# Scan scores as two 64-row products side by side instead of one 128-row product with zeros

## The chip, the core and the metric

One core of a Trainium2 chip runs the whole program. The metric is the device time of one execution in microseconds (us); the number compared is the median of several runs. TensorE is called PE, its weight loads PEld, VectorE is DVE, ScalarE is ACT, GpSimd is POOL and SyncE, which issues the DMAs, is SP.

## The reference, cut to what matters

The program is two layers of a diffusion backbone over 512 latent tokens and 256 context tokens of width 1024: SwiGLU blocks around a token mixer, RWKV-7 in the first layer and Hyena in the second. The change touches the recurrence of RWKV-7 alone. It has 16 heads of 64 channels, and runs once forwards and once backwards:

```python
def step(S, inp):
    w_t, k_t, v_t, kk_t, ka_t = inp[:5]
    sa = jnp.einsum('dbhvk,dbhk->dbhv', S, kk_t)
    S = S * w_t[..., None, :] - sa[..., None] * ka_t[..., None, :] + v_t[..., None] * k_t[..., None, :]
    if r is None:
        return S, None
    return S, jnp.einsum('dbhvk,dbhk->dbhv', S, inp[5])
```

Everything is in float32.

## The kernel before, in words

The recurrence is done in chunks of 64 tokens. Within a chunk the steps become small matrices: for each head, all products of a scaled kk or r at one token with a scaled ka or k at another, called scores here, the inverse of a triangular matrix made of them, and the state carried from chunk to chunk. `rwkv_prep` writes the scaled vectors to DRAM (`S_A` from the tile `AR`, `S_K` from `KD`), and `rwkv_scan` reads them back and does the rest.

- The 12 chunks (4 of context, then 8 latent) are taken two at a time as a block, for each of two directions d: 12 blocks. The 16 heads are two groups g of 4 pairs of heads (index `p_`). One block has thus 4 items (g and chunk), and the scan has 48 items.
- `load(i)` (L1124) fetches for one block and group the tiles `AG` (kk and r side) and `KK` (ka and k side). In both, a pair of heads takes the 128 partitions, one head in each half (`hr[0]`, `hr[1]`). In `AG` each head hh has columns of its own, and its values stand in the partitions of its half; the other half is filled with zeros (L1140 on ACT for the first `NZ` = 4 loads, L1142 on POOL for the other 20, two instructions each). A 128x4 memset (L1136, POOL) for loads 2 to 9 sets the place in the order from which such a load may go. There are 10 buffers of `AG`.
- `stage_a` (L1191) makes the scores of one item: for each of the 4 pairs one matmul (L1211) with `KK` as the weights, 128 rows by 128 columns, and both heads' columns of `AG` streaming; the zeros keep the heads apart. For a latent chunk `ns` is 2 (kk and r) and 256 columns stream; for a context chunk `ns` is 1 and 128 do. So there are 32 items with 256 columns and 16 with 128. The hardware runs each float32 matmul as two instructions, each with its weight load.
- The scores lie in PSUM: in a tile `sc` of two banks of a pool with one buffer, or, in the 11 items that are scored ahead of the first solve (`lead`), two times out of three in one of the two banks of `ps`. `evac` then has ACT copy them: half a tile to `Bc` (L1219), the other half over the zeros of `AG` (L1187), and part to `Hu` (L1187); POOL masks the last two with an affine select (L1188).
- From `Bc` DVE inverts the triangles (L1240, L1258 to L1278, L1290, L1308) with small matmuls L1317 and L1328 in between. Per item then come `rhs` (L1357, L1365), `solve` (L1372), `advance` (L1382, L1388, L1395), `carry` (POOL L1348 scales the state `Sn`, DVE L1350 copies it into `SV`) and `keys` (transposes, L1174).
- The loop at the end of `rwkv_scan` sets the order: at step n it issues solve, rhs, the scores of the item LA = 11 steps ahead, pieces of inversions, advance and so on. PE and DVE keep this written order throughout the scan, POOL while n is negative; ACT, SP and later POOL are ordered by the scheduler from its own estimate.

Of the kernel before, what the change touches and what calls it, by code (L numbers as in the profile page):

```python
# [9 lines left out]
F32 = mybir.dt.float32  # L10
F32R = mybir.dt.float32r
I32 = mybir.dt.int32
AF = mybir.ActivationFunctionType
# [5 lines left out]
P = 128  # L19
# [7 lines left out]
NP = 4  # L27
# [20 lines left out]
NVEC = 2  # L48
NL = 0
ML = {ET.PE, ET.DVE, ET.Pool}  # L50
NZ = 4
NLD = 2
FIRST = {"AG", "KK", "Bc", "L", "Dl"}
NBG = (1, 1, 2)
# [222 lines left out]
class K:  # L277
# [819 lines left out]
    def rwkv_scan(self, cx, po):  # L1097
        nc = self.nc

        pools = [self.pool(n, 1, cx) for n in ("sfirst", "schk")]  # L1100
        hr = [slice(0, 64), slice(64, P)]
# [4 lines left out]
        def T(shape, tag, bufs=1):  # L1106
            return pools[tag not in FIRST].tile(shape, F32, tag=tag, name=self.nm(tag), bufs=bufs)
# [18 lines left out]
        def load(i):  # L1126
            t, g = pairs[i]
            d = t["d"]
            ch = min(t["chs"])
            x = (g, d, ch // 6)  # L1130
            c = slice(ch % 6, ch % 6 + 2)
            AG = T([P, 2, 2, NP, 2, 64], "AG", RING)
            KK = T([P, 2, NP, 2, 64], "KK", 2)

            if NLD <= i < RING:
                nc.gpsimd.memset(AG[:, :, :, 0, 0, 0:1], 0.0)  # L1136
            for hh in range(2):
                z = AG[hr[1 - hh], :, hh].rearrange("p c a s t -> p c (a s t)")
                if i < NZ:
                    nc.scalar.activation(z, self.ones[hr[1 - hh]].unsqueeze(2).to_broadcast([64, 2, NP * P]), AF.Copy, scale=0.0)  # L1140
                else:
                    nc.gpsimd.memset(z, 0.0)  # L1142
                nc.sync.dma_start(
                    AG[hr[hh], :, hh].rearrange("p c a s t -> p c (a s t)"),
                    self.S_A[x][c, hr[hh]].rearrange("c p a s t -> p c (a s t)"),
                )
            nc.sync.dma_start(
                KK.rearrange("p c a s t -> p c (a s t)"), self.S_K[x][c].rearrange("c p a s t -> p c (a s t)")
            )
            t.setdefault("ld", {})[g] = (ch, AG, KK)  # L1150
# [35 lines left out]
        def causal(dst, src, d, ns, base):  # L1186
            nc.scalar.copy(dst, src)  # L1187
            nc.gpsimd.affine_select(  # L1188
                out=dst, in_=dst, compare_op=ALU.is_ge, fill=0.0, base=base,
                pattern=[[0, NP], [1, ns], [1 if d == 0 else -1, 64]], channel_multiplier=-1 if d == 0 else 1,  # L1190
            )  # L1191


        def stage_a(t, g, ci, lead):
            d = t["d"]
            ch = t["chs"][ci]
            ch0, AG, KK = t["ld"][g]
            c = ch - ch0
            u = 2 * g + ci
            ns = 2 if ch < 8 else 1  # L1200
            if u == 0:
                t["Bc"] = T([P, 4, NP, 64], "Bc", 3)
                t["ops"] = {}
            Bc = t["Bc"]
            Hu = T([P, NP, 64], "Hu", RKT) if ns == 2 else None
            if lead and count[0] % 3:
                sc = self.ps().rearrange("p (a h s t) -> p a h s t", a=NP, h=2, s=1)
            else:
                sc = self.psc.tile([P, NP, 2, 2, 64], F32, tag="sc", name=self.nm("sc"))
            for p_ in range(NP):  # L1210
                nc.tensor.matmul(  # L1211
                    sc[:, p_, :, :ns, :], KK[:, c, p_].rearrange("p s t -> p (s t)"), AG[:, c, :, p_, :ns, :],
                    start=True, stop=True,
                )
            t["ops"][g, ci] = (AG[:, c], Hu)

            def evac(hh):
                h_, o_ = hr[hh], hr[1 - hh]
                nc.scalar.copy(Bc[h_, u], sc[h_, :, hh, 0, :])  # L1219
                causal(AG[o_, c, hh, :, :ns], sc[o_, :, hh, :ns, :], d, ns, -1)  # L1220
                if ns == 2:
                    causal(Hu[h_].unsqueeze(2), sc[h_, :, hh, 1:2, :], d, 1, 0)

            for hh in range(2):
                ev.append(lambda hh=hh: evac(hh))
# [306 lines left out]
        count = [0, 0]  # L1532

        def scores(lead):
            x = next(nxt, None)
            if x is not None:
                count[0] += 1
                while count[1] < 2 * N and 2 * count[1] < count[0] + LDA:
                    load(count[1])
                    count[1] += 1  # L1540
                stage_a(*x, lead)


        def item(n, ahead=0):
            k, c = divmod(n, 4)
            d, g = divmod(c, 2)
            pos = k - d + ahead
            return (lines[d][pos][0], g, lines[d][pos][1]) if 0 <= pos < M and n >= 0 else None

        while count[1] < NLD:  # L1550
            load(count[1])
            count[1] += 1
# [5 lines left out]
        for n in range(-LA, 4 * M + 5):  # L1558
# [8 lines left out]
            p, x = item(n - 1), item(n)  # L1567
# [41 lines left out]
            if (n + IO) % 4 == UQ and block(n + IO):  # L1609
                t = block(n + IO)  # L1610
# [3 lines left out]
            if (n + LA + 1) % 4 == 0 and block(n + LA):  # L1614
                t = block(n + LA)
# [509 lines left out]
```

## Time and profile before

| what | value |
|---|---|
| median of 3 runs | 3029.62 us (3029.31 to 3033.85) |
| the profiled execution: its own time | 3036.99 us |
| the profiled execution: its span, first to last instruction | 3035.0 us |
| mean granted clock of TensorE in it | 0.947 |
| busy share of PE, DVE, ACT, POOL | 92%, 60%, 38%, 16% |
| the scan, first score to the start of the last inversion | about 1004 to 1381 us of the span |

A busy share is a mean over stages: the blocks before and after the scan are long streams of matmuls, in which PE alone counts. The scan is another kind of stage, and is read by itself, from windows cut out of the span. A granted clock of 1.0 is 2.4 GHz, 0.5 is 1.2 GHz; a number between is a mean over time at both.

### The profile page before, as it was taken

Reading aid. Unit: us, or ns where it says so; the run is one execution under the profiler, and the core shown is the slowest. Engines: PE = TensorE matmul, PEld = TensorE weight load, DVE = VectorE, ACT = ScalarE, POOL = GpSimd, SP = SyncE. Lnnn points to the kernel's source line nnn. Section 1 sums busy time; section 2 is a strip of 40 time slices with the busy share of each in tenths; the row PEclk is TensorE's granted clock in tenths of the full one; section 3 lists DMA queues with packets and bytes.
Section 4 is the critical chain, followed back from the end, with each engine's and each line's share of the span. In section 5 each row is a group of like instructions: output and inputs, shape, how many; then the busy total and the mean of one; then the engine's idle time right before and its main releaser. Section 6 shows DMA issues by size and latency. Waiting matters only on the chain.

```text
span 3035.0 us, 46673 instructions
## 1 busy us (share of the span) xinstructions
PE 2782.4 (92%) x18394; PEld 2324.9 (77%) x18394; DVE 1818.3 (60%) x3403; ACT 1163.4 (38%) x2007; POOL 477.7 (16%) x647
## 2 busy tenths in 40 slices
PE   8899999978889378887899999999999989899998
PEld 4788888857666366765788889888887777888888
DVE  4656444474798688997655546455365588653334
ACT  3221121255666678874232223322334322332222
POOL 0000000032343445532100000000000054100000
PEclk9999999979989678998899999999999999999999
DMA  5434333313688744434345543455333544232331
GB/s 206 155 106 148 132 128 109 100 37 102 171 211 209 192 117 130 125 86 125 128 146 167 171 162 112 140 183 180 106 116 135 206 143 147 105 124 85 97 106 48
DMA packets 363971, 409.36 MB, mean 135 GB/s; under 512 B 77719, under 2 KB 303127, under 8 KB 362024
## 3 DMA queue, kind: packets, MB, share of 16 engines
q1 hardware_dynamic: 363752, 406.39, 42.4%
q8 instruction: 144, 2.36, 0.3%
q14 instruction: 75, 0.61, 0.1%
HBM read 340.20 MB, written 65.34 MB: 134 GB/s over the span
## 4 chain that ended last, share of the span: by engine, by line
PE 74%; DVE 13%; DMA 4%; ACT 3%; issue 3%; POOL 2%; SPq 0%; DVEq 0%; POOLq 0%; ACTq 0%
PE ps L481 21%; PE ps L482 21%; PE ps L483 21%; DVE Dl L1278 1%; PE sc L1211 1%; DVE wlo L487 1%; DVE Tm L1271 1%; DMA mraw<-in_mod_wt 1%; DVE SV L1350 1%; DVE zt L1946 1%; POOL za L1947 1%; DVE zl L487 1%; PE pf L1759 1%; DMA AG<-S_A 1%; DMA x<-in_xT 1%
## 5 line engine op out<-in xcount | busy, mean ns | idle before, releaser
L482 PE MATMUL ps<-hl,whi 128*128 128x512 f32 (+1 forms) x2064 | 742.4, 362 | 3.5 <-DVE hl L268 3.5
L481 PE MATMUL ps<-hh,whi 128*128 128x512 f32 (+1 forms) x2064 | 732.2, 363 | 14.2 <-ACT hh L267 10.7
L483 PE MATMUL ps<-hh,wlo 128*128 128x512 f32 (+1 forms) x2064 | 735.6, 362 | 2.0 <-DVE wlo L487 2.0
L487 DVE TENSOR_TENSOR wlo<-raw,whi 128x1024 fp32r<-128x1024 f32 (+1 forms) x325 | 392.9, 1215 | 383.6 <-ACT whi L486 382.6
L486 ACT CAST whi<-raw 128x1024 fp32r<-128x1024 f32 (+1 forms) x338 | 344.6, 1028 | 707.8 <-PE ps L482 631.2
L481 PEld LDWEIGHTS ps<-hh,whi 128*128 128x128 f32 x2064 | 386.7, 190 | 78.3 <-ACT hh L267 13.2
L482 PEld LDWEIGHTS ps<-hl,whi 128*128 128x128 f32 x2064 | 392.8, 190 | 64.4 <-DVE hl L268 4.9
L483 PEld LDWEIGHTS ps<-hh,wlo 128*128 128x128 f32 x2064 | 391.8, 190 | 63.4 <-DVE wlo L487 2.9
L481 PE MATMUL ps<-dh,whi 128*128 128x512 f32 (+1 forms) x1072 | 354.3, 336 | 7.8 <-DVE x L660 7.8
L482 PE MATMUL ps<-dl,whi 128*128 128x512 f32 (+1 forms) x1072 | 358.3, 335 | 0.0
L483 PE MATMUL ps<-dh,wlo 128*128 128x512 f32 (+1 forms) x1072 | 357.8, 335 | 0.0
L421 DVE CUSTOM_DVE_ANT_0 mraw<-mraw,mc 128x1024 f32<-128x1024 f32 x128 | 156.5, 1223 | 142.8 <-DMA mraw<-in_mod_wt 141.6
L481 PEld LDWEIGHTS ps<-dh,whi 128*128 128x128 f32 x1072 | 203.5, 190 | 29.4 <-DVE x L660 8.0
L482 PEld LDWEIGHTS ps<-dl,whi 128*128 128x128 f32 x1072 | 204.2, 190 | 20.5
L483 PEld LDWEIGHTS ps<-dh,wlo 128*128 128x128 f32 x1072 | 204.0, 190 | 20.2
L375 POOL COPY mraw<-dl 128x1 f32<-128x1 f32 x128 | 44.8, 364 | 896.3 <-DVE dl L487 631.2
L611 DVE TENSOR_TENSOR sg<-sg,ps 128x512 f32<-128x512 f32 (+1 forms) x110 | 69.1, 633 | 175.6 <-PE ps L483 165.5
L610 ACT ACTIVATE sg<-ps 128x512 f32<-128x512 f32 (+1 forms) x110 | 59.8, 553 | 209.7 <-PE ps L483 202.8
L486 ACT CAST dh<-sg 128x512 fp32r<-128x512 f32 (+1 forms) x110 | 62.1, 575 | 201.2 <-DVE sg L611 201.1
L482 PE MATMUL ps<-xl,whi 128*128 128x512 f32 (+2 forms) x336 | 125.8, 376 | 9.6 <-DVE xl L811 7.1
L481 PE MATMUL ps<-xh,whi 128*128 128x512 f32 (+2 forms) x336 | 123.6, 380 | 9.5 <-issue 5.9
L483 PE MATMUL ps<-xh,wlo 128*128 128x512 f32 (+2 forms) x336 | 123.2, 372 | 0.0
(315 smaller groups left out, 4498.6 us busy)
## 6 DMA issues: line engine op xcount, KB each, us to landing
raw<-in_wgu SPq DMA_DIRECT2D x88, 1024.0 KB, 5.0
mraw<-in_mod_wt SPq DMA_DIRECT2D x128, 512.0 KB, 5.3
raw<-in_wd SPq DMA_DIRECT2D x24, 1024.0 KB, 5.0
raw<-in_wrkv SPq DMA_DIRECT2D x12, 1024.0 KB, 5.9
S_A<-AR SPq DMA_DIRECT2D x32, 384.0 KB, 3.6
AG<-S_A SPq DMA_DIRECT2D x48, 256.0 KB, 4.2
KK<-S_K SPq DMA_DIRECT2D x24, 512.0 KB, 4.5
KL<-S_K SPq DMA_DIRECT2D x48, 256.0 KB, 2.9
```

What stands on the lines that cost most here:

```text
L375: self.nc.gpsimd.tensor_copy(raw[:, :1], held)
L421: nc.vector.tensor_tensor_reduce(dst, raw, self.rows[w], 1.0, 0.0, ALU.mult, ALU.add, accum_out=cols[w][:, m : m + 1])
L481: nc.tensor.matmul(out, wh, xh, start=start, stop=False)
L482: nc.tensor.matmul(out, wh, xl, start=False, stop=False)
L483: nc.tensor.matmul(out, wl, xh, start=False, stop=stop)
L486: self.nc.scalar.copy(hi, src)
L487: (self.nc.gpsimd if pool else self.nc.vector).tensor_tensor(lo, src, hi.bitcast(F32), ALU.subtract)
L610: nc.scalar.activation(sg, pg, AF.Silu)
L611: nc.vector.tensor_mul(sg, sg, pu)
L1211: nc.tensor.matmul(sc[:, p_, :, :ns, :], KK[:, c, p_].rearrange("p s t -> p (s t)"), AG[:, c, :, p_, :ns, :], start=True, stop=True,)
L1271: nc.vector.tensor_tensor(tm[:, js, rs], L[:, p, rs].unsqueeze(1).to_broadcast([P, n, w]), Dl[:, js, p : p + 1].to_broadcast([P, n, w]), A ...
L1278: nc.vector.tensor_tensor(Dl[:, js, rs], Dl[:, js, rs], tm[:, js, rs], ALU.subtract)
```

## The change

The zeros are no longer written. Each score product becomes two, one for each head: 64 rows of `KK` as weights (still 128 columns) and that head's 64 rows of `AG` streaming. The two heads use different row halves of PE's array and write to different PSUM banks. In `sc` the bank is now the head; ahead of the first solve every second item takes both banks of `ps` and the others take `sc`.

```diff
-NZ = 4
             for hh in range(2):
-                z = AG[hr[1 - hh], :, hh].rearrange("p c a s t -> p c (a s t)")
-                if i < NZ:
-                    nc.scalar.activation(z, self.ones[hr[1 - hh]].unsqueeze(2).to_broadcast([64, 2, NP * P]), AF.Copy, scale=0.0)
-                else:
-                    nc.gpsimd.memset(z, 0.0)
                 nc.sync.dma_start(
...
-            if lead and count[0] % 3:
-                sc = self.ps().rearrange("p (a h s t) -> p a h s t", a=NP, h=2, s=1)
+
+            if lead and count[0] % 2:
+                sc = [self.ps().rearrange("p (a s t) -> p a s t", a=NP, s=2) for _ in range(2)]
             else:
-                sc = self.psc.tile([P, NP, 2, 2, 64], F32, tag="sc", name=self.nm("sc"))
+                sc = self.psc.tile([P, 2, NP, 2, 64], F32, tag="sc", name=self.nm("sc"))
+                sc = [sc[:, hh] for hh in range(2)]
             for p_ in range(NP):
-                nc.tensor.matmul(
-                    sc[:, p_, :, :ns, :], KK[:, c, p_].rearrange("p s t -> p (s t)"), AG[:, c, :, p_, :ns, :],
-                    start=True, stop=True,
-                )
+                for hh in range(2):
+                    nc.tensor.matmul(
+                        sc[hh][:, p_, :ns, :], KK[hr[hh], c, p_].rearrange("p s t -> p (s t)"),
+                        AG[hr[hh], c, hh, p_, :ns, :], start=True, stop=True,
+                    )
...
-                nc.scalar.copy(Bc[h_, u], sc[h_, :, hh, 0, :])
-                causal(AG[o_, c, hh, :, :ns], sc[o_, :, hh, :ns, :], d, ns, -1)
+                nc.scalar.copy(Bc[h_, u], sc[hh][h_, :, 0, :])
+                causal(AG[o_, c, hh, :, :ns], sc[hh][o_, :, :ns, :], d, ns, -1)
                 if ns == 2:
-                    causal(Hu[h_].unsqueeze(2), sc[h_, :, hh, 1:2, :], d, 1, 0)
+                    causal(Hu[h_].unsqueeze(2), sc[hh][h_, :, 1:2, :], d, 1, 0)
```

The change moves instructions at the start of the scan, where the scheduler and the PSUM buffers decide. In the changed kernel all line numbers after `load` are lower by 3 to 6 (L1211 is L1208 there).

PE, the first scores; `pq` are products of the end of the preparation, `ps` and `sc` scores, and the number after the underscore is the tile. Before:

```order
L1211 MATMUL ps_8339<-AG_8322,KK_8323 128x128 x4
L1211 MATMUL ps_8350<-AG_8322,KK_8323 128x128 x4
L1075 MATMUL pq_8282<-rb_8253,rks_8283 128x384
L1075 MATMUL pq_8282<-r_8094,rks_8283 128x384
L1211 MATMUL sc_8361<-AG_8329,KK_8330 128x2x64 x4
```

and in the change:

```order
L1074 MATMUL pq_8282<-rb_8253,rks_8283 128x384
L1074 MATMUL pq_8282<-r_8094,rks_8283 128x384
L1208 MATMUL ps_8335<-AG_8322,KK_8323 128x64
L1208 MATMUL ps_8336<-AG_8322,KK_8323 128x64
L1208 MATMUL ps_8335<-AG_8322,KK_8323 128x64
L1208 MATMUL ps_8336<-AG_8322,KK_8323 128x64
L1208 MATMUL ps_8335<-AG_8322,KK_8323 128x64
L1208 MATMUL ps_8336<-AG_8322,KK_8323 128x64
L1208 MATMUL ps_8335<-AG_8322,KK_8323 128x64
L1208 MATMUL ps_8336<-AG_8322,KK_8323 128x64
L1208 MATMUL sc_8351<-AG_8322,KK_8323 128x64 x8
```

The last `pq` products now stand ahead of the first scores, one item takes both `ps` tiles, and the next takes `sc`. In the steady part of the scan PE's order is the same, with 8 matmuls where 4 stood.

SP, the DMAs around the first load (`AG` and `KK` are loads of the scan; `S_A`, `S_K` and `S_b` are the last writes of the preparation). Before:

```order
L1143 DMA AG_8322<-S_A_4902 64x2x512
L1058 DMA S_A_4905<-AR_8250 128x6x128
L1065 DMA S_K_4913<-KD_8255 64x6x64
L1143 DMA AG_8322<-S_A_4902 64x2x512
L1147 DMA KK_8323<-S_K_4910 128x2x512
L1143 DMA AG_8329<-S_A_4906 64x2x512
L1079 DMA S_b<-rb_8150 128x128
L1143 DMA AG_8329<-S_A_4906 64x2x512
```

and in the change:

```order
L1137 DMA AG_8322<-S_A_4902 64x2x512
L1078 DMA S_b<-rb_8150 128x128
L1057 DMA S_A_4905<-AR_8250 128x6x128
L1064 DMA S_K_4913<-KD_8255 64x6x64
L1062 DMA S_K_4913<-KD_8255 64x6x128
L1064 DMA S_K_4913<-KD_8255 64x6x64
L1137 DMA AG_8322<-S_A_4902 64x2x512
L1141 DMA KK_8323<-S_K_4910 128x2x512
```

The second half of the first `AG` load and its `KK` have moved behind `S_b` and two more writes of `S_K`.

## Rows read from the trace of the kernel before

**Rows 1.** The page: the chain that ended last, shares of the span by engine.

```profile
PE 74%; DVE 13%; DMA 4%; ACT 3%; issue 3%; POOL 2%; SPq 0%; DVEq 0%; POOLq 0%; ACTq 0%
```

**Rows 2.** Windows of the scan: length, busy PE, PEld, DVE, ACT, POOL, then PEclk, DMA.

```profile
993.00:1069.00 76.00, 35.56 (x348) 32.13 (x348) 47.08 (x152) 47.57 (x102) 30.57 (x62) 0.63 0.67 182
...
1131.00:1193.00 62.00, 51.17 (x782) 41.78 (x780) 53.80 (x162) 49.52 (x110) 31.31 (x50) 0.83 0.43 122
1193.00:1257.00 64.00, 54.75 (x979) 45.52 (x975) 57.67 (x168) 53.65 (x119) 34.45 (x54) 0.95 0.45 128
1257.00:1318.00 61.00, 52.33 (x1016) 43.74 (x1015) 56.58 (x167) 52.88 (x118) 33.23 (x52) 1.00 0.46 134
```

**Rows 3.** Waits of DVE and of ACT from 1069 to 1381: total us, times, longest.

```profile
DVE SV L1350 <- POOL Sn L1348: 6.7, 9, 0.9
DVE Sn L1388 <- PE pss L1382: 4.8, 6, 2.5
...
ACT Bc L1219 <- PE sc L1211: 19.1, 14, 2.5
```

**Rows 4.** The chain: start, us, what; then issues of line 1143, min/median/max ns.

```profile
993.58 1.05 ACT AG L1140
...
997.94 0.60 ACT a L1030
...
999.10 4.99 DMA AG<-S_A
...
L1143 SPq DMA_DIRECT2D AG<-S_A x48: 573/599/897, 994.0 to 1279.4; - x48
```

**Rows 5.** The chain: scores (first and last of 11 with x8), and starts of blocks.

```profile
1082.23 2.01 PE sc L1211 x8
...
1159.79 1.07 DVE L L1290
...
1193.07 1.09 DVE L L1290
...
1287.49 1.07 DVE L L1290
...
1317.63 1.07 DVE L L1290
...
1335.60 1.92 PE sc L1211 x8
...
1349.30 1.08 DVE L L1290
```

**Rows 6.** Timeline of PE from 1268: start, us, line, operation; one item.

```profile
1268.29 0.69 PE L1382 MATMUL pss<-SV,KT 128*64 128x64 f32 x16
1268.90 0.68 PE L1395 MATMUL psy<-Hu,SV 64*64 64x64 f32 x16
...
1271.79 1.99 PE L1211 MATMUL sc<-AG,KK 128*128 128x256 f32 x8
1273.72 1.20 PE L1328 MATMUL ps<-XT,Dlo 32*32 32x32 f32 x64
```

**Rows 7.** Groups by line and form from 990 to 1460: busy us, mean ns, idle before.

```profile
L1142 POOL MEMSET AG<- 64x1024 f32 x40 | 38.7, 967 | 8.9 <-PE pss L1357 7.1 <-PE psy L1365 0.3
...
L1372 PEld LDWEIGHTS pss<-RHS,XT 64*64 64x64 f32 x768 | 31.7, 154 | 23.1 <-issue 8.9 <-POOL Sn L1348 6.8 <-ACT XT L1330 3.4
...
L1382 PEld LDWEIGHTS pss<-SV,KT 128*64 128x64 f32 x768 | 29.1, 149 | 19.9 <-ACT SV L1374 11.9 <-issue 5.6 <-ACT RHS L1359 1.0
...
L1140 ACT ACTIVATE AG<-ones 64x1024 f32<-64x1024 f32 x8 | 8.4, 1053 | 2.2 <-POOL selg L1566 2.1
```

**Rows 8.** The copies of line 1350: min/median/max ns; then two pieces of the timeline.

```profile
L1350 DVE COPY SV<-Sn x88: 275/292/1345, 1068.4 to 1423.0; 64x256 f32<-64x256 f32 x88
...
1150.02 1.98 POOL L1142 MEMSET AG<- 64x1024 f32 x2
1150.57 1.57 DVE L1350 COPY SV<-Sn 64x256 f32<-64x256 f32 x2
```

## The prediction

> **What bounds the kernel now.** I read the page's chain of waits first: 74% of the span is PE and 13% is DVE [rows 1]. The PE share is the long products before and after the scan, which the change leaves alone. So I cut the scan out with windows [rows 2]. There no engine is full, but DVE is nearest to it: from 1193 to 1318 it is busy 57.67 + 56.58 = 114.3 us of 125, against 107.1 for PE and 106.5 for ACT. In the start of the scan, 993 to 1069, all engines are half empty: there loads and their order set the pace. The list of waits says what ends DVE's and ACT's idle time [rows 3]: DVE waits for the scaled state from POOL (6.7 us) and for the state product of PE (4.8 us), and ACT waits 19.1 us for the scores, 14 times. Last comes the chain in order of time [rows 5]: from 1082 to 1336 it runs through the scores in 11 long pieces, about one in each block of four items, 25.5 us together. The reader is to see a loop in which PE, ACT, POOL and DVE take turns, with DVE short of idle time and the scores on the path once in four times.
>
> The sum below is made against the profiled execution, 3036.99 us (3035.0 of span and 2 around it). The median of the runs shown is 3029.62, 7.4 lower; I carry the difference over to the median.
>
> **Scores of latent chunks (32 items).** One takes 8 instructions with 256 columns each; the first starts at 1271.79 and the next group at 1273.72, so 1.93 us at full clock [rows 6]. No row shows two products in the row halves of the array. The nearest are the products of line 1382, which use the two column halves, and line 1395, which use opposite quarters: 16 instructions of 64 columns in 1268.90 - 1268.29 = 0.61 us, so 8 steps of two at a time. Between 8 steps of 64 columns and 8 of 256 lie 1.32 us, 0.86 ns a column. Eight steps of two products with 128 columns then take 0.61 + 8 x 64 x 0.86 ns = 1.05 us. That is the low end; the high end is no pairing at all, in the rivals. I take the low end because both rows of line 1382 and 1395 show pairs, in unlike positions of the array. An item saves 0.88 us, 32 items 28 us of PE.
>
> What of this lies on the path: the 11 pieces of 25.5 us [rows 5], of which 0.88/1.93 = 46% goes, 11.6 us. The rest is beside other work. Not all of the 11.6 stays gained: behind the scores comes ACT with its copies, and DVE, which has only 10.7 us idle in 125 [rows 2], so 2.7 us for a block of about 31, from which I'd take 1.1. Part of that idle time ends with POOL's scaled state [rows 3], which is late next and does not come from the scores. **I take 8 us; ends 0 and 11.6.**
>
> **Scores of context chunks (16 items).** Before, 128 columns stream over weights of 128 columns; by the line above this is 1.05 us. Now 64 stream, but the weights still have 128 columns, and each has to be loaded before its product. If the weights set the pace it stays at 1.05, if the streaming does it falls to 0.61. They stand at the start, where the chain is made of loads [rows 4]. **I take 0**; the better end, 16 x 0.44 = 7 us of PE, would lie beside those loads.
>
> **The zeros on POOL.** 40 memsets of 967 ns go, 38.7 us [rows 7]. POOL is busy about half of the time [rows 2], so their cover is POOL's own idle time. One effect reaches DVE: its copies of the state take 292 ns in the median, but with memsets beside them two took 1.57 us instead of 0.58 [rows 8]; I found three such places (1150, 1207, 1215) with DVE on the chain. **I take 2 us; ends 0 and 4.**
>
> **The zeros on ACT, and the order at the start.** Of the 8 activates of 1053 ns [rows 7] four stand on the chain from 993.58 to 997.94, 4.4 us, ahead of the last step of the preparation [rows 4]. They go. Against this, three more issues of SP (S_b and two of S_K) now stand ahead of the second half of the first load and of its KK; at 0.6 us each [rows 4] that is 1.8 us on the load for which PE waits. The last products of the preparation now stand ahead of the first scores on PE; whoever waits for them delays all scores, though their input comes earlier too, since ACT is free. In the part ahead of the first solve two sets of banks alternate where there were three places, so an item can wait for ACT's copies of the item before the last. **I take -2 us for all of it**; the ends are -4.4 (only the activates) and +5 (one load of 4.99 us [rows 4] that comes too late once). The 128x4 memsets and the affine selects stay.
>
> **After the scan** the scheduler has swapped some matmuls and DMAs of the feed-forward part. I take 0, with the spread of the runs shown, some 4 us, as its ends.
>
> **Sum.** -8 - 2 - 2 = -12 us: 3025 for the profiled execution, **3018 us for the median**. What a measurement of this kernel can tell from no change is about 0.2%, 6 us.
>
> **Rivals.**
>
> *Weights one after the other (the change does not do what it says).* All pairs in the trace have column ranges of their own; here two products share the columns and differ in rows. Were they taken in turn, 16 steps with weights of 128 columns would take 16 x 1.05/8 = 2.1 us: 0.17 more than before for a latent item, 1.05 more for a context item. That is 11 x 0.17 = 2 us on the path and 16 x 1.05 = 17 us at the start, from none to all of it beside the loads; with the 4 us of the zeros gained, -2 to +15, and I put it at +3: 3033. For it speaks that a load of 64 rows is not shorter than one of 128 [rows 7]: 154 ns on line 1372 against 149 on line 1382. Against it, loads of two products do run at once on both lines, or 16 could not fit into 0.61 us [rows 6]. The Trainium skill, page "TensorE: Matmul & The Clock Gate", section LDWEIGHTS, says that a load's time goes with its columns and not with its rows, so that halving the rows buys nothing. By that rule the 16 loads cost twice what the 8 did unless two of them overlap; the trace agrees with the rule on the length of a load.
>
> *The clock falls (ends slower).* In 1257 to 1318 the granted clock is 1.00, at 1131 to 1193 it is 0.83 [rows 2], and it is at 0.63 in the start, where PE is busy less than half of the time. The change takes 0.88 us of PE from each item of about 7.7. From 1193 to 1318 PE's busy time would go from 107.1 us to about 93 of 125, 74%. If the stretch from 1193 to 1349 fell to 0.83, its five blocks, 156.2 us, would go like the block from 1159.79 to 1193.07, 33.3 us each [rows 5]: 5 x 33.3 - 156.2 = 10 us more. The slower matmuls would then eat what the scores gain, and with 4 us from the zeros the time is 3036. It decides once the clock of that stretch is at 0.83 or below. For it speaks that the stretch from 1131, with PE 83% busy, had no full clock; against it, those 83% contain the matmuls that the slow clock itself had stretched, so the two shares are not alike. The same page says, in Part 1, that the throttled clock is the default and activity releases it. The fall at the start agrees with that.
>
> *Off the path.* DVE's idle time is short pauses, and the copies of ACT wait for something else as soon as the scores are early. Then only the 4 us of the zeros remain: 3026. For it speaks DVE at 91% [rows 2]; against it, 19.1 us of ACT's waits are for the scores alone [rows 3].
>
> *More than forecast.* POOL, ACT and PE all get lighter, and the loop takes all of DVE's idle time: 2.7 us for each of ten blocks: 3003.
>
> **How the numbers follow.** The forecast's own case (3009 to 3026): 0.57; more than forecast 0.07; weights in turn 0.11; off the path 0.11; the clock 0.14. Faster by over 0.2%, below 3023.6: 0.53 of the forecast, 0.07, and 0.02 of off the path: 0.62. Within 0.2%: 0.04 of the forecast, 0.05 of weights in turn, 0.09 of off the path, 0.04 of the clock: 0.22. Slower: 0.06 of weights in turn, 0.10 of the clock: 0.16. The range is 3003 to 3032: it leaves out the far end of the better case and most of the two slower ones, some 0.18.
>
> **What would show it.** Right: the scores of a latent item take 16 instructions in about 1.05 us at full clock, starting in twos; the scores' pieces on the chain halve; ACT waits for them about 10 us instead of 19; the state's copies fall to 0.3 us where memsets stood; the starts of line 1290 come about 30 us apart where they are 31.2 now; the granted clock of 1193 to 1318 stays at 0.95 or above. Wrong: 16 instructions in 1.9 us or more (weights in turn); a clock at 0.83 there (the clock); scores halved but blocks as long as before, with DVE's or ACT's waits under other names (off the path); a first score later than 1004.

## The result, and the profile after

| what | value |
|---|---|
| changed kernel, median of 4 runs | 3058.17 us (3054.68 to 3066.61) |
| kernel before, 4 runs beside it | 3029.47 us (3028.59 to 3033.85) |
| ratio | 1.0092, 95% interval 1.0072 to 1.0113 |
| profiled execution after: own time, span, clock | 3057.56 us, 3055.8 us, 0.935 |

The change makes the kernel 28.7 us slower. The forecast was 3018, its range ended at 3032, and none of its cases reached 3058.

The scores themselves did what was forecast. In PE's timeline after (start, us, line, operation; a shown duration reaches past the next start) the item of [rows 6] looks like this:

```profile
1287.14 1.16 PE L1208 MATMUL sc<-AG,KK 64*128 64x128 f32 x16
1288.23 1.20 PE L1325 MATMUL ps<-XT,Dlo 32*32 32x32 f32 x64
```

From the first score to the next group it is 1.09 us (1.93 before). In the trace the 16 instructions start in twos, 7 ns apart, a pair every 0.11 us. The copies of the state, by line (min/median/max ns; [rows 8] has the kernel before), have lost the cases in which a memset of the zeros stood beside them:

```profile
L1347 DVE COPY SV<-Sn x88: 275/291/731, 1065.7 to 1449.5; 64x256 f32<-64x256 f32 x88
```

Before, five copies beside a memset took 1023 to 1026 ns. The longest of [rows 8], 1345 ns, is none of them: it stood beside a product of POOL that the change leaves (before):

```profile
1383.83 1.28 POOL L1455 TENSOR_TENSOR pv<-pv,psq 128x512 f32<-128x512 f32 x1
1383.90 2.47 DVE L1350 COPY SV<-Sn 64x256 f32<-64x256 f32 x2
```

Run 9 below, without zeros, has it again (1343 ns).

The time went into the latent blocks. The additions of the state, 44 in each kernel, mark the scan's main part. Their line shows it (before, then after; first and last start in us):

```profile
L1388 DVE TENSOR_TENSOR Sn<-pss,Sn x44: 402/418/426, 1092.1 to 1433.8; 128x256 f32<-128x256 f32 x44
```

```profile
L1385 DVE TENSOR_TENSOR Sn<-pss,Sn x44: 396/424/426, 1088.8 to 1459.3; 128x256 f32<-128x256 f32 x44
```

From first to last it takes 370.5 us where it took 341.7, 28.8 us more. This stretch is called **the loop** below. The two profiled spans differ by 20.8 us only, because what comes ahead of the loop is 3.3 us shorter and what comes behind it 4.7 us. Both are within what single profiles differ by (over the profiles of all the runs below, the first addition comes at 1085.8 to 1098.0 us, and 1591.3 to 1601.2 us pass from the last to the end), so the loss lies in the loop, to a few us. The blocks lengthen from about 1193 on: L1287 (L1290 before, [rows 5]) starts at these two places, five blocks apart, 36.3 us each, where the blocks of [rows 5] are 31.2 apart from 1193.07 to 1349.30:

```profile
1193.51 1.06 DVE L1287 STREAM_TRANSPOSE L<-Dl 128x512 f32<-128x512 f32 x1
...
1374.77 1.05 DVE L1287 STREAM_TRANSPOSE L<-Dl 128x512 f32<-128x512 f32 x1
```

The windows that answer to [rows 2] (length, busy PE, PEld, DVE, ACT, POOL, PEclk, DMA) show PE, DVE, ACT and POOL less busy from 1131 on, DVE too, which was nearly full:

```profile
993.00:1069.00 76.00, 45.46 (x460) 39.47 (x460) 47.28 (x154) 38.81 (x92) 18.97 (x50) 0.50 0.64 178
...
1131.00:1193.00 62.00, 48.21 (x852) 41.79 (x854) 51.48 (x153) 48.37 (x107) 26.31 (x44) 0.77 0.38 111
1193.00:1257.00 64.00, 46.64 (x889) 40.42 (x884) 47.81 (x141) 45.53 (x102) 22.51 (x40) 0.79 0.43 124
1257.00:1318.00 61.00, 47.16 (x896) 41.53 (x896) 48.51 (x142) 43.38 (x95) 19.96 (x35) 0.80 0.41 114
```

So it is waiting, not work. The waits from 1069 to 1381 that answer to [rows 3] (total us, times, longest):

```profile
DVE Sn L1385 <- PE pss L1379: 19.5, 11, 3.1
DVE Sn L1385 <- ACT AG L1181: 12.5, 6, 2.2
DVE SV L1347 <- POOL Sn L1345: 12.4, 9, 4.0
...
ACT XT L1297 <- DVE L L1287: 17.4, 8, 3.3
ACT gw L485 <- DMA gr<-in_g: 16.9, 9, 4.3
ACT Bc L1216 <- PE sc L1208: 12.8, 9, 2.4
```

Two of these waits of ACT before:

```profile
ACT XT L1300 <- DVE L L1290: 10.3, 10, 2.0
...
ACT gw L486 <- DMA gr<-in_g: 4.9, 7, 1.6
```

ACT's wait for the scores fell from 19.1 to 12.8 us, towards the 10 of the forecast. Grown are its waits for DVE's transpose (10.3 to 17.4 us) and for a DMA (4.9 to 16.9), and DVE's for PE's state product (4.8 to 19.5), for POOL's scaled state (6.7 to 12.4) and for ACT. One place shows how these hang together. ACT from 1266, then PE, then DVE:

```profile
1266.62 0.58 ACT L1170 COPY KT<-ps 128x512 f32<-128x512 f32 x1
1269.57 2.50 ACT L1297 COPY XT<-L 32x512 f32<-32x512 f32 x4 [2.36 <-DVE L L1287]
1272.08 0.37 ACT L1433 COPY gr<-ps 128x256 f32<-128x256 f32 x1
1272.35 0.77 ACT L1371 ACTIVATE SV<-pss 64x256 f32<-64x256 f32 x2
```

```profile
1266.98 0.68 PE L1369 MATMUL pss<-RHS,XT 64*64 64x64 f32 x16
...
1268.68 1.16 PE L1208 MATMUL sc<-AG,KK 64*128 64x128 f32 x16
1273.17 1.12 PE L1379 MATMUL pss<-SV,KT 128*64 128x64 f32 x16 [3.33 <-ACT SV L1371]
```

```profile
1268.42 1.07 DVE L1287 STREAM_TRANSPOSE L<-Dl 128x512 f32<-128x512 f32 x1
...
1274.41 0.42 DVE L1385 TENSOR_TENSOR Sn<-pss,Sn 128x256 f32<-128x256 f32 x1 [2.21 <-ACT AG L1181]
```

PE has the solve (L1369) done at 1267.66. ACT is idle from 1267.2, but the next in its order is the XT copy, which waits for DVE's transpose, ends at 1272.07, and has the SV copies of that solve behind it. So SV starts 4.7 us after its input is there, PE stands still for 3.33 us, and DVE behind PE. (The releaser named last on DVE is ACT; by PE's row it is the state product at 1273.17.)

Before, SV stood ahead. ACT at the same place of a latent block in the kernel before:

```profile
1285.76 0.59 ACT L1176 COPY KT<-ps 128x512 f32<-128x512 f32 x1
1286.24 0.38 ACT L1436 COPY gr<-ps 128x256 f32<-128x256 f32 x1
1286.51 0.77 ACT L1374 ACTIVATE SV<-pss 64x256 f32<-64x256 f32 x2
1288.60 2.52 ACT L1300 COPY XT<-L 32x512 f32<-32x512 f32 x4 [1.32 <-DVE L L1290]
1291.15 0.37 ACT L1359 COPY RHS<-pss 128x256 f32<-128x256 f32 x1
```

The program does not write this order; the scheduler makes it. Two more groups moved in each latent block: the gate's casts `gw`, which wait for a DMA, went from behind the copies of an item's scores to ahead of them, and all four copies `Dl` (L1232) went ahead of the two copies L1327, which had stood between them two and two. On POOL the scaling of `Sn` (L1345) moved behind selects that it had stood ahead of (shown with run 12).

### The profile page after: what moved, and what is told of

The parts are those of the page before. It is cut to its first block, busy times and chain, and to the rows that moved or that the text cites. A ratio compares the mean times of both kernels' runs of the same rounds, so it can differ in the third digit from the quotient of the medians.

```text
span 3055.8 us, 47366 instructions
## 1 busy us (share of the span) xinstructions
PE 2782.9 (91%) x18778; PEld 2336.2 (76%) x18778; DVE 1813.8 (59%) x3403; ACT 1156.2 (38%) x1999; POOL 441.9 (14%) x607
## 5 line engine op out<-in xcount | busy, mean ns | idle before, releaser
L480 PE MATMUL ps<-hh,whi 128*128 128x512 f32 (+1 forms) x2064 | 733.9, 363 | 12.8 <-ACT hh L266 10.5
L486 DVE TENSOR_TENSOR wlo<-raw,whi 128x1024 fp32r<-128x1024 f32 (+1 forms) x325 | 393.2, 1216 | 375.9 <-ACT whi L485 374.8
L1275 DVE TENSOR_TENSOR Dl<-Dl,Tm 128x126 f32<-128x126 f32 (+22 forms) x372 | 122.3, 329 | 7.3
```

What stands on the lines that cost most here:

```text
L480: nc.tensor.matmul(out, wh, xh, start=start, stop=False)
L486: (self.nc.gpsimd if pool else self.nc.vector).tensor_tensor(lo, src, hi.bitcast(F32), ALU.subtract)
L1275: nc.vector.tensor_tensor(Dl[:, js, rs], Dl[:, js, rs], tm[:, js, rs], ALU.subtract)
```

## The experiments

Each ratio is to the kernel before, run beside it on the same chip; 1% is 30 us. "Loop" is the time from the first to the last addition of the state in the profiled execution, one for each kernel, so good to a few us.

| run | what it has | median us | ratio (95%) | loop us |
|---|---|---|---|---|
| | kernel before | 3029.5 to 3032.5 | 1 | 341.7 |
| | changed kernel | 3058.17 | 1.0092 (1.0072 to 1.0113) | 370.5 |
| 1 | change, groups on ACT back by kind | 3045.89 | 1.0050 (1.0037 to 1.0062) | 352.9 |
| 2 | before, XT and Dl moved as in the change | 3067.08 | 1.0111 (1.0095 to 1.0127) | 378.9 |
| 3 | change with zeros | 3064.31 | 1.0111 (1.0097 to 1.0125) | 374.8 |
| 4 | change, XT alone back | 3041.09 | 1.0033 (1.0022 to 1.0045) | 356.1 |
| 5 | run 1 and POOL: Sn first | 3042.28 | 1.0033 (1.0021 to 1.0045) | 350.0 |
| 6 | run 1, scores twice | 3045.99 | 1.0044 (1.0029 to 1.0059) | 358.2 |
| 7 | run 4 and POOL: Sn first | 3040.96 | 1.0033 (1.0021 to 1.0046) | 355.9 |
| 8 | change, ACT as written | 3051.20 | 1.0059 (1.0042 to 1.0077) | 356.4 |
| 9 | change, ACT and POOL exactly as before | 3029.84 | 0.9998 (0.9988 to 1.0009) | 339.1 |
| 10 | before, ACT and POOL exactly as the change | 3070.07 | 1.0135 (1.0118 to 1.0153) | 378.5 |
| 11 | run 9, scores twice | 3037.95 | 1.0016 (1.0005 to 1.0027) | 345.4 |
| 12 | change, ACT exactly as before | 3040.12 | 1.0026 (1.0016 to 1.0037) | 348.2 |
| 13 | change, POOL exactly as before | 3063.73 | 1.0101 (1.0086 to 1.0116) | 373.2 |
| 14 | run 9, XT behind RHS | 3030.53 | 0.9995 (0.9982 to 1.0008) | 340.6 |
| 15 | before, XT behind RHS | 3030.62 | 0.9995 (0.9984 to 1.0006) | 338.2 |

An order is changed by edges that make one instruction issue behind another of its engine and wait for nothing else:

```diff
+    def behind(self, inst, ins):
+        self.tc.add_manual_dep(
+            inst.ins, ins.ins.name,
+            mybir.DependencyInfo(mybir.DependencyClass.NoSync, mybir.DependencyReason.DATA), reason="behind",
+        )
```

**Runs 1 to 4** set the order of ACT against the clock of PE, which had fallen too, and against the missing zeros. Run 1, with `last` and `Es` holding the instructions written last:

```diff
-                nc.scalar.copy(XTc[r, :, b : b + 32], t["XD"][r])
+                xc = nc.scalar.copy(XTc[r, :, b : b + 32], t["XD"][r])
+                if "SV" in last:
+                    self.behind(xc, last["SV"])
...
+                if hb > 1 and "oo" in last:
+                    self.behind(dc, last["oo"])
...
+                    if len(Es) > 3:
+                        self.behind(self.cast, Es[-3])
```

> The changed kernel with ACT's order of the kernel before, by order-only edges that wait for nothing: the four XT copies behind the two SV copies of solve, two of the four Dl copies behind the XT copies of L1328, the gate's casts behind the scores' copies. Theory A (ACT's order: what ACT now has ahead of the SV and score copies holds up the loop): the loss goes, the latent blocks take 31 us or less instead of 36, the granted clock of 1193 to 1349 is back at 0.90 or above, and the time is between 3010 and 3032 us, 3018 as forecast if the rest of the forecast holds. Theory B (the clock: shorter scores leave PE too idle, the clock falls, and everything on PE is slower): the order changes nothing of it, the clock of 1193 to 1349 stays near 0.80 and the time within 3050 to 3062 us.

Run 2 writes XT ahead of the solve in the kernel before, and the edges the other way round:

```diff
+            while early:
+                early.pop(0)()
             if p:
                 solve(*p)
...
+                if "X" in last:
+                    self.behind(sc_, last["X"])
...
+                    if "D" in last:
+                        self.behind(oc, last["D"])
```

> The kernel before, its 128-row products and zeros unchanged, with ACT's order of the changed kernel: the XT copies ahead of the SV copies of solve, the four Dl copies ahead of the XT copies of L1328. The gate's casts are left where they were. Theory A: slower than the kernel before by 15 to 30 us, so 3045 to 3060, latent blocks of 34 to 36 us, and DVE waiting for POOL and for pss as in the changed kernel. Theory B: PE has all its old work, so the clock stays at 0.95 or above from 1193 to 1318 and the time is 3030 us, within 5.

Run 3 puts the zeros' two instructions back into `load`:

```diff
+                if i < NZ:
+                    nc.scalar.activation(z, self.ones[hr[1 - hh]].unsqueeze(2).to_broadcast([64, 2, NP * P]), AF.Copy, scale=0.0)
+                else:
+                    nc.gpsimd.memset(z, 0.0)
```

> The changed kernel with the zeros still written as before, on ACT for the first 4 loads and on POOL for the rest; nobody reads them. ACT's order in the latent blocks is that of the changed kernel. Theory A: as slow as the changed kernel, 3058 us, plus what the zeros cost, 2 to 4 us: 3056 to 3064. Theory B: the same 3056 to 3064. A third theory, that the loss comes from the zeros' absence (POOL runs ahead, the start of the scan is ordered otherwise): 3022 to 3035.

Run 4 has the first three added lines of run 1 alone.

> The changed kernel with the XT copies alone put behind the SV copies of solve; the Dl copies and the gate's casts stay where the change put them. Theory A: the XT copies wait for DVE's transpose with the SV copies behind them, 14 us of waiting in 6 places, and are the larger part: 3030 to 3043 us, latent blocks of 32 to 34 us. If the gate's casts, which wait for a DMA ahead of the score copies, are the larger part: 3045 to 3056. Theory B: 3050 to 3062.

Measured: 3045.89, 3067.08, 3064.31 and 3041.09 us. Run 2 has the old products, the zeros and the whole of PE's old work, and is slower than the changed kernel: theory B falls, though the loss is larger than the 15 to 30 us of theory A. Run 3 is no faster with the zeros, so their absence is not the cause; its ACT order in the latent blocks is that of the changed kernel but for a few copies, so it is the new products, with their banks, that made the scheduler turn the order. Run 4 wins back some 18 us with one edge. But run 1 missed 3032 by 14 us, its clock from 1193 to 1349 is 0.86 and not 0.90, and its two further edges won nothing over run 4: either what was left was no order, or the orders were not yet alike.

**Runs 5 to 8.** What is left: POOL's order (5, 7), the clock (6), or any order that deviates (8). Run 5 on top of run 1, run 7 on top of run 4 (`held` are the selects of the second half of the scores of this step):

```diff
             nc.gpsimd.tensor_tensor(Sn, Sn, pc.to_broadcast([P, NP, 64]), ALU.mult)
+            while held:
+                self.behind(held.pop(), scaled)
```

> The first run (ACT's order back, 3045.9 us) with one more set of order-only edges, on POOL: the affine selects of the second half of a step's scores stand behind the scaling of Sn of the same step, as they mostly did before the change. Theory A2 (what is left of the loss, 15 us, is POOL's order, which the change moved too: Sn behind selects that wait for ACT's copies; DVE waits 8.9 us for Sn from 1121 to 1345 where it waited 5.8): 3038 us or less, and DVE's wait for Sn below 5 us. Theory B (the clock holds what is left): 3043 to 3049 us, the clock from 1193 to 1381 as in the first run, 0.81 to 0.89.

> The run with the XT copies alone moved back (3041.1 us), with POOL's edges of the other run added. Theory A2: 3026 to 3035 us, the best so far. Theory B: within 4 of 3041.

Run 6 on top of run 1:

```diff
-            for p_ in range(NP):
+            for p_ in [p for p in range(NP) for _ in range(ns)]:
```

> The first run (ACT's order back, 3045.9 us) with each score product of a latent chunk issued twice in a row, the second over the first, so that PE's work is about what it was before the change (2.2 us for an item, 1.93 before). Theory B: PE busy again, the clock of 1193 to 1318 goes from 0.81 and 0.89 back to 0.95 or above, and the time falls although there is more work: 3028 to 3040 us. Theory C (PE's length is on the path at either clock, the forecast's own price of 0.88 us on 11 of 32 items): 8 to 14 us slower than the first run, 3053 to 3060.

Run 8:

```diff
-MS = {ET.PE, ET.DVE}
+MS = {ET.PE, ET.DVE, ET.Activation}
```

> The changed kernel with ACT kept in written order throughout the scan, as PE and DVE are: XT behind SV, the gate's casts ahead of SV two items later than now, the Dl copies behind those of the keys. If any order that has XT behind SV does (theory A): 3030 to 3045 us. If the casts stand in the way ahead of SV: above 3050.

Measured: 3042.28, 3040.96, 3045.99, 3051.20 us. Sn first gains at most some 5 us in run 5 and nothing in run 7, and DVE's wait for Sn in run 5 is 8.0 us, not below 5: these edges were not POOL's old order. Run 6 fell between its two theories: some 35 us more of PE work (32 items of 1.1) cost nothing and gained nothing, at a clock of 0.90 from 1193 to 1318 (0.85 in run 1). The scheduler also moved some copies and selects in it, so it is not run 1 with more work alone. Run 8 is just above the 3050 for casts in the way: DVE waits 11.6 us for them from 1121 to 1345, but also 16.5 for Sn (5.8 before), so the casts are not singled out. None settled what was left, so the next runs took the orders whole.

**Runs 9 to 11.** Every copy of ACT and every select, scaling and XT memset of POOL in the scan is chained in the order of the other kernel, letter by letter from a string:

```diff
+        def chain(e, order):
+            q, last = seq[e], None
+            for k in order:
+                i = q[k].pop(0)
+                if last is not None:
+                    self.behind(i, last)
+                last = i
...
         drain(bg)
+        chain("act", ORD_A)
+        chain("pool", ORD_P)
```

> The changed kernel with the orders of ACT and of POOL in the scan both exactly those of the kernel before (a chain of order-only edges through all copies, and through all selects, scalings and XT memsets); PE and DVE keep their written order. What differs from the kernel before in the scan is the score products, the zeros and a few loads. Theory A (the two orders are the whole loss and the forecast's sum holds otherwise): 3012 to 3026 us, first to last addition of the state (44 of them) in 335 us or less, where the kernel before has 342, the first run 353 and the changed kernel 370. Theory D (the orders are some 20 us of it; what the shorter products save, the lower clock of PE takes back, so that 8 to 12 us of loss remain): 3036 to 3046 us, 348 to 354 us, clock from 1131 to 1381 between 0.75 and 0.88.

> The kernel before, products and zeros unchanged, with the orders of ACT and of POOL in the scan exactly those of the changed kernel (POOL's zeros stand where the scheduler puts them); PE's and DVE's instructions stand as in the kernel before, one for one. Theories A and D: slower by 18 to 32 us, 3048 to 3064, first to last state addition 360 to 375 us. Theory B (order plays no part): 3030 us, within 5.

> The run with both orders of the kernel before, and each score product of a latent chunk issued twice. 32 items get 1.1 us of PE work more. If PE's length is on the path at a fixed clock: 8 to 14 us slower than that run. Theory D: within 4 us of it, with the clock from 1131 to 1381 higher by 0.05 or more.

Measured: 3029.84 us, 0.9998 of the kernel before; 3070.07, 1.0135; 3037.95, 1.0016. Run 10 is the cleanest: PE and DVE have the same instructions in the same order as the kernel before, and the two orders alone cost 1.35%, 41 us, more than the 18 to 32 expected. The waits that grow from 1121 to 1345 are those of the changed kernel: of PE, in the kernel before, in the changed kernel, in run 10, in run 9:

```profile
PE pss L1382 <- ACT SV L1374: 4.6, 3, 2.2
...
PE pss L1357 <- DVE Sn L1388: 3.1, 2, 1.9
```

```profile
PE pss L1379 <- ACT SV L1371: 23.1, 7, 5.0
PE pss L1354 <- DVE Sn L1385: 12.6, 7, 3.2
```

```profile
PE pss L1403 <- ACT SV L1395: 18.8, 7, 4.0
...
PE pss L1378 <- DVE Sn L1409: 10.1, 6, 2.4
```

```profile
PE pss L1400 <- ACT SV L1392: 11.0, 6, 3.2
...
PE pss L1375 <- DVE Sn L1406: 4.5, 4, 1.8
```

With the orders back (run 9), the loss is gone, but the forecast gain does not come: the time lies between its two theories, and the interval allows 4 us of gain at most. Run 10 is also slower than the changed kernel, by 0.43% or 13 us, with intervals apart: at the new orders the old products and zeros cost about what the forecast had put on them, at the old orders nothing that shows. How much of the 13 us is the zeros is not resolved, since run 3 (1.0111) lies between the two. What the shorter products are worth thus hangs on the orders.

Where the 0.88 us of each item stay is read from 1121 to 1345, in windows (columns as above) and in the groups of PE (busy us, mean ns). The kernel before, run 9, run 11:

```profile
1121.00:1345.00 224.00, 190.77 (x3282) 158.08 (x3278) 200.49 (x585) 184.73 (x409) 116.07 (x180) 0.92 0.43 122
```

```profile
1121.00:1345.00 224.00, 179.53 (x3534) 156.38 (x3536) 198.05 (x588) 185.52 (x410) 92.22 (x156) 0.85 0.41 122
```

```profile
1121.00:1345.00 224.00, 190.22 (x4016) 168.82 (x4014) 201.06 (x593) 184.92 (x409) 92.57 (x158) 0.94 0.42 123
```

```profile
L1211 PE MATMUL sc<-AG,KK 128*128 128x256 f32 x224 | 60.9, 419 | 5.0 <-POOL Sn L1348 3.2 <-POOL Hu L1188 1.7 <-issue 0.2
```

```profile
L1229 PE MATMUL sc<-AG,KK 64*128 64x128 f32 x448 | 38.1, 318 | 6.6 <-ACT Hu L1202 6.4
```

```profile
L1229 PE MATMUL sc<-AG,KK 64*128 64x128 f32 x888 | 60.8, 290 | 6.0 <-ACT Hu L1202 5.9
```

The scores take 22.8 us less in 28 items, but PE as a whole is only 11.2 us less busy: all its other work takes 11.6 us more, 141.4 for 129.9 or 9%, at a granted clock of 0.85 for 0.92, whose ratio is 8%. The other half is idle time of PE. DVE and ACT do as much as before (198 and 186 us of 224). In run 11 the doubled scores bring PE's busy time back to 190 us and the clock to 0.94, and cost 8 us in all by the medians, 5.5 by the ratios: between theory D's 4 and the 8 to 14 of work on the path. So, in these three profiles, a shorter PE comes with a lower clock and a longer PE with a higher one, and about half of the saving or of the added work is taken up in this way.

**Runs 12 to 15.** Which order, and what more is in it. Runs 12 and 13 chain one engine alone:

```diff
-        chain("pool", ORD_P)
```

> The changed kernel with ACT's order in the scan exactly that of the kernel before, POOL left to the scheduler. If ACT's order is the whole of it and the first run only missed its details (XT behind the RHS copy in some blocks): 3027 to 3034 us, as with both orders. If POOL's order holds what the first run left: 3038 to 3046.

> The changed kernel with POOL's order in the scan exactly that of the kernel before, ACT left to the scheduler, which keeps XT ahead of SV in the latent blocks. If POOL's order holds a part of its own: 3040 to 3050 us. If ACT's order is the whole of it: 3053 to 3062.

Runs 14 and 15 change the string: in five blocks XT goes behind the RHS copy.

```diff
+ORD_A = ORD_A.replace("SSXXXXR", "SSRXXXX")
```

> The run with both orders of the kernel before, and in the five blocks where the XT copies stand between SV and the RHS copy they go behind the RHS copy too. The RHS copy then no longer waits for DVE's transpose (4.7 us of waiting in 6 places and 2.5 us of copies in each of the five): 2 to 8 us faster than that run, 3022 to 3028. If the RHS copy is not waited for there: the same, 3030.

> The kernel before, with its own orders of ACT and POOL held by the same chain, and the XT copies behind the RHS copy in the same five blocks. If the gain is the order's alone: 2 to 8 us faster than the kernel before, 3022 to 3028, and equal to the run before it in this list. If the shorter scores are worth something at the better order: slower than that one by 3 or more.

Measured: 3040.12, 3063.73, 3030.53 and 3030.62 us. ACT's order alone wins back 1.0092 - 1.0026 = 0.66%, 20 us. POOL's alone wins back nothing, but on top of ACT's it is worth another 1.0026 - 0.9998 = 0.28%, 8 us, and with it the loss is accounted for. What POOL's order does can be seen at one place (the kernel before, then after):

```profile
1190.39 0.67 POOL L1188 TENSOR_SCALAR_AFFINE_SELECT AG<-AG 64x512 f32<-64x512 f32 x1 [8.38 <-ACT AG L1187]
1191.14 0.68 POOL L1348 TENSOR_TENSOR Sn<-Sn,PC 128x256 f32<-128x256 f32 x1
1191.77 0.45 POOL L1188 TENSOR_SCALAR_AFFINE_SELECT Hu<-Hu 64x256 f32<-64x256 f32 x1
```

```profile
1190.05 0.66 POOL L1182 TENSOR_SCALAR_AFFINE_SELECT AG<-AG 64x512 f32<-64x512 f32 x1 [8.39 <-ACT AG L1181]
1190.78 0.45 POOL L1182 TENSOR_SCALAR_AFFINE_SELECT Hu<-Hu 64x256 f32<-64x256 f32 x1
1191.21 0.61 POOL L1345 TENSOR_TENSOR Sn<-Sn,PC 128x256 f32<-128x256 f32 x1
```

After, the scaling, for which DVE waits with the next SV copies, has one select more ahead of it. Whether these half microseconds add up to the 8 us is argued, not shown: DVE's wait for Sn is no longer in run 12 than in run 9 (4.0 and 5.6 us).

Runs 14 and 15 gained nothing over run 9 and the kernel before: the copy RHS is not waited for there. No version beat the kernel before by what its measurement can tell.

## Why the prediction was wrong

**The latent scores, -8 us.** The size was right: 1.05 us forecast, 1.09 measured, in pairs in the row halves as on the nearest rows. So the rival of weights in turn (2.1 us) falls. The Trainium skill, page "TensorEngine Tiling (Array Packing)", section Tiling Modes, says that different tiles can load and multiply in parallel; these 16 instructions in 1.09 us agree. But the step from PE's saving to the path failed. With the orders of before the path got no shorter (run 9). I read the 11 pieces of [rows 5] as time that the path would lose. (The first of them, at 1082.23, is a context item with 128 columns; without it the 11.6 us would have been 10.7.) Half of the saving went back through the clock, and the rest became idle time of PE, between DVE and ACT that had as much to do as before. At the orders of before, that is close to the rival "off the path" (3026), with a lower clock beside it. The same page of the Trainium skill, section Performance Considerations, warns that tiling shortens PE and not the copies out of PSUM; here ACT copies one item's scores for 2.7 us (1263.88 to 1266.60 in the changed kernel) where PE now computes them in 1.1.

**No term for the moved orders: the step that failed.** The sum had terms for the order at the start and after the scan. For the latent blocks I had looked at PE's order, found it the same, and stopped, although ACT, SP and later POOL are ordered by the scheduler from its own estimate. ACT's list of instructions had the move in it: XT, which waits for DVE, ahead of SV, for which PE waits. By [rows 2] DVE had nearly no idle time, so a place where ACT waits for DVE and PE for ACT could be expected to cost. The runs put 20 us on ACT's order and 8 us on POOL's: the 28.7 us, with the rest of the change at about 0 once the orders are back. What made the scheduler choose the new orders is known only so far as run 3 goes: the new products and their banks do it without the zeros' absence.

**The clock's rival** (3036, decides at 0.83 or below). The clock did fall, to 0.79 and 0.80, and its condition was met; but as what began the loss it is out. Run 10 has PE's old work and loses 41 us, and run 9 has a clock of 0.85 and loses none. From 1193 to 1318 the clock was 0.97 before, 0.86 with the new orders alone (run 10), 0.85 with the new products alone (run 9) and 0.80 with both, so waiting and shorter work each bring it down by about as much. What the lower clock adds to the loss at the new orders is not separated. The page "TensorE: Matmul & The Clock Gate" of the Trainium skill, Part 1, calls the throttled clock the default state that activity releases; run 11 agrees, with 0.94 for 0.85 when the scores are doubled.

**The zeros, -2 and -2.** The copies stretched beside memsets are gone, as forecast; the longest one of [rows 8] had another cause. The first addition of the state comes 3.3 us earlier, which single profiles do not resolve. In time, run 3 and the changed kernel differ by 0.19%, with intervals that overlap: not resolved either.

**Context scores, 0.** Nearly right: two items start at 1002.29 and 1004.02, 1.73 us apart, at a granted clock of 0.50; before, at 0.50 too, 1.84 (1018.29 to 1020.13). The estimate of 1.05 us at full clock was somewhat long: half of 1.84 is 0.92.

**After the scan, 0.** From the last addition of the state to the end it is 1596.5 us of the profiled span where it was 1601.2: 0.7 us outside the 4 us that I gave it, and within what single profiles differ by.

## What to carry to other kernels

Where a scheduler orders some engines, changing the cost of one instruction can turn the order of another engine: list that order before and after for every engine, not only for those whose code changed, and look for an instruction that waits for a busy engine and now stands ahead of one that PE waits for. To tell an order from the work, force the old order onto the new work and the new order onto the old work; the two crossed runs (0.9998 and 1.0135) settled what the lists of waits could not. And work taken from PE in a loop bound by other engines can come back as a lower granted clock (here 0.85 for 0.92).

## What the runs showed of the hardware that was not expected

PE's busy time hardly follows its work here: with scores of 60.9, 38.1 and 60.8 us from 1121 to 1345 PE is busy 190.8, 179.5 and 190.2 us, at clocks of 0.92, 0.85 and 0.94. I had expected a lower clock to follow a saving on PE as an accident of one stage; here it took about half of both changes of PE's work, one in each direction.

A copy of the state on DVE that starts 0.05 to 0.21 us behind the start of a POOL instruction ends 0.14 to 0.15 us behind the end of that instruction, in all 12 copies over 0.72 us of the trace before: 1.02 to 1.03 us beside memsets, 0.73 to 0.76 beside selects of 0.66, 1.12 and 1.35 beside products of 1.04 and 1.28, where the median is 0.29. So the selects and products that the change leaves stretch copies too, and taking the memsets away takes away only the cases of 1.02 us.
